# Value products per key block with 128 weight columns, and normalisation shared with the scalar engine, in the attention of a two-block layer

## The chip, the cores and the metric

One Trainium2 chip, one core of it. The metric is the time of one execution in device microseconds (us), the median of several runs. TensorE (PE) does the products, VectorE (DVE), the scalar engine (ACT) and GpSimd (POOL) the elementwise work, SyncE (SP) issues the DMAs. Reads of weights into TensorE are shown as PEld.

## The reference, cut to what matters

The input x has 512 rows (positions) and 1024 columns, all in float32. A first block (retention and differential attention) is followed by a second one, in which the change lies. The second block has eight heads "a" of dilated window attention and eight heads "b" of latent attention, each with values of 64 columns. Both come down to the same thing: scores of 512 queries against the keys up to their own position, a table of biases or of the causal mask added, softmax over the keys, and the product of the probabilities with the values.

```python
s = scores + table                       # (heads, 512, 512), causal
p = softmax(s, axis=-1)
o = einsum('hqk,khd->qhd', p, v)         # d = 64
mixed = concat([o_a * silu(z_a), o_b * silu(z_b)])
out = x + mixed @ w_out                  # 1024 x 1024
```

The softmax in the kernel subtracts the row's largest score, takes the exponential, sums it, and multiplies with the reciprocal of the sum. silu(z) is computed as 0.5 z (1 + tanh(z/2)); the kernel carries the 0.5 elsewhere.

## The kernel before, in words

**Numbers in two parts.** TensorE reads float32 operands here as a rounded format (fp32r). To keep float32 accuracy each operand is split into a high part (a rounded copy, made by the scalar engine) and a low part (what is left, made by VectorE by a subtraction): `split`, L266 to L268. A product of two such operands takes three matmuls, high x high, high x low and low x high: `mm3`, L304 to L307. Weights come by DMA as raw tiles and are split by the `Streamer` (L107 to L154): ACT makes the high part (L135), VectorE or GpSimd the low part (L137). GpSimd does it for the keys in `POOL_LO` (L51).

**The loop over steps.** In the second block a step is one tile of 128 queries (t = 0 to 3) of one head; the 16 heads come in the order of `SEQ` (L45): four "a", eight "b", four "a". In step s the loop (L1356 to L1366) issues

- `probs` (L1208): the scores of step s (t+1 blocks of 128 keys: width n of 128, 256, 384 or 512), their addition to the table with the row's extremum on VectorE (L1219), the exponential with its sum on ACT (L1222), the reciprocal (L1224) and the normalisation with a factor 0.5 on VectorE (L1225);
- at t = 1 and t = 2 the query and key stacks of the head after this one (`ready_q`, `ready_k`): transposes of normalised projections and their split into tiles of a ring with the tag "qk", 12 tiles long. A pair of "a" heads takes 2 + 4 tiles, a "b" head 4;
- `fill` up to half a step's share: pieces of dense work (projections, gates, the output projection) from a list, by a planned cost in columns against a due amount;
- `probs_T` (L1228) of step s-2: transposes of the normalised probabilities on TensorE (t+1 blocks), and their split into a high and a low tile per step;
- `fill` up to the full share;
- `weigh` (L1239) of step s-3: the value products. For each of the t+1 key blocks three matmuls with the values as weights (64 columns) and 128 columns of transposed probabilities, summed in a PSUM tile of 64 x 512 for the head. At t = 3 ACT copies that tile into one half of a 128 x 512 tile; after two heads `mix_in` (L1255) multiplies it with the gate and splits it for the output projection `project` (L1278).

TensorE's order in this loop is the order in which the program issues (`manual_schedule`, L891); the order on the other engines is laid by a planner at build time, which knows the dependencies but not the measured durations. Each engine works its queue in order. PSUM has three tiles for dense work (`ps_d`), two for transposes (`ps_t`), two for scores (`ps_s`) and one for value products (`ps_o`). One tile with the tag "th" is shared by the gates' tanh (L361) and the mix.

`mla_q` (L1070) makes the queries of the latent heads with a root mean square over 64 and over 32 columns per head; `mla_kv` (L1094) and `dil_v` (L1158) make the value tiles, a high and a low one each.

## Time and profile before

| | |
|---|---|
| time, median of 3 runs | 939.8 us (937.45 to 940.37) |
| the profiled execution, its own time | 939.06 us |
| its span in the trace | 936.7 us, 13702 instructions |
| TensorE (matmul) busy | 916.1 us, 98% of the span |
| weight loads (PEld) busy | 777.0 us, 83% |
| VectorE busy | 555.9 us, 59% |
| ACT busy | 452.7 us, 48% |
| GpSimd busy | 209.0 us, 22% |
| mean granted clock of TensorE | 0.996 of full speed |

The profile is of one execution. A row of the trace names the line of the kernel, the engine, the operation and the tiles written and read (out<-in). Matmuls are pipelined: the shown duration of one (0.22 us for 128 columns) is longer than the distance between the starts of two that follow each other, and the distance is what a product costs. The loop over steps fills the trace from about 705 us to 920 us; `project(2)` follows.

### The profile page before, as it was taken

Reading aid. Unit: us, or ns where it says so; the run is one execution under the profiler, and the core shown is the slowest. Engines: PE = TensorE matmul, PEld = TensorE weight load, DVE = VectorE, ACT = ScalarE, POOL = GpSimd, SP = SyncE. Lnnn points to the kernel's source line nnn. Section 1 sums busy time; section 2 is a strip of 40 time slices with the busy share of each in tenths; the row PEclk is TensorE's granted clock in tenths of the full one; section 3 lists DMA queues with packets and bytes.
Section 4 is the critical chain, followed back from the end, with each engine's and each line's share of the span. In section 5 each row is a group of like instructions: output and inputs, shape, how many; then the busy total and the mean of one; then the engine's idle time right before and its main releaser. Section 6 shows DMA issues by size and latency. Waiting matters only on the chain.

```text
span 936.7 us, 13702 instructions
## 1 busy us (share of the span) xinstructions
PE 916.1 (98%) x5113; PEld 777.0 (83%) x5113; DVE 555.9 (59%) x1223; ACT 452.7 (48%) x923; POOL 209.0 (22%) x236
## 2 busy tenths in 40 slices
PE   9999999999999999999999999999997999999998
PEld 6788887777888888888888888888996788999886
DVE  5443342347764555668665345344649897778884
ACT  5311331345555544666565433233545667666650
POOL 3001100116111133411310000132347453341100
PEclk9999999999999999999999999999999899999999
DMA  7474230322433423222332234633423121211412
GB/s 247 124 221 141 66 89 27 91 71 64 136 113 113 157 91 91 91 91 91 124 113 68 70 110 135 203 127 127 141 63 97 39 80 46 68 47 47 158 45 90
DMA packets 70099, 96.20 MB, mean 103 GB/s; under 512 B 5336, under 2 KB 46184, under 8 KB 70034
## 3 DMA queue, kind: packets, MB, share of 16 engines
q1 hardware_dynamic: 70034, 95.34, 32.5%
q8 instruction: 40, 0.66, 0.3%
q14 instruction: 25, 0.20, 0.1%
HBM read 86.91 MB, written 11.03 MB: 105 GB/s over the span
## 4 chain that ended last, share of the span: by engine, by line
PE 88%; DVE 6%; DMA 2%; ACT 2%; POOL 1%; issue 1%; SPq 0%; ACTq 0%; DVEq 0%
PE dps L305 9%; PE dps L307 9%; PE dps L306 9%; PE tps L305 7%; PE tps L307 7%; PE tps L306 7%; PE aps L305 2%; PE aps L306 2%; PE aps L307 2%; PE dop L823 2%; PE ppt L1231 2%; PE ops L305 2%; PE yps L307 2%; PE yps L305 2%; PE yps L306 2%; PE ops L306 2%
## 5 line engine op out<-in xcount | busy, mean ns | idle before, releaser
L137 DVE TENSOR_TENSOR wl<-wr,wh 128x1024 fp32r<-128x1024 f32 (+2 forms) x113 | 139.6, 1236 | 121.4 <-ACT wh L135 117.4
L135 ACT ACTIVATE wh<-wr 128x1024 fp32r<-128x1024 f32 (+1 forms) x132 | 137.7, 1043 | 147.4 <-DMA wr<-in_w_in_dram 46.9
L305 PE MATMUL dps<-h1h,wh 128*128 128x512 f32 x320 | 128.3, 401 | 0.0
L307 PE MATMUL dps<-h1h,wl 128*128 128x512 f32 x320 | 125.3, 392 | 0.0
L306 PE MATMUL dps<-h1l,wh 128*128 128x512 f32 x320 | 125.1, 391 | 0.0
L305 PE MATMUL tps<-wh,h1h 128*128 128x512 f32 x256 | 103.3, 404 | 3.0 <-ACT dqn L366 2.4
L307 PE MATMUL tps<-wh,h1l 128*128 128x512 f32 x256 | 101.3, 396 | 0.0
L306 PE MATMUL tps<-wl,h1h 128*128 128x512 f32 x256 | 100.2, 392 | 0.3 <-DVE wl L137 0.3
L307 PEld LDWEIGHTS dps<-h1h,wl 128*128 128x128 f32 x320 | 60.1, 188 | 13.0
L306 PEld LDWEIGHTS dps<-h1l,wh 128*128 128x128 f32 x320 | 60.2, 188 | 12.0 <-issue 0.5
L305 PEld LDWEIGHTS dps<-h1h,wh 128*128 128x128 f32 x320 | 60.2, 188 | 11.8
L305 PEld LDWEIGHTS tps<-wh,h1h 128*128 128x128 f32 x256 | 48.2, 188 | 14.7 <-ACT dqn L366 4.1
L307 PEld LDWEIGHTS tps<-wh,h1l 128*128 128x128 f32 x256 | 48.1, 188 | 11.0 <-DVE h1l L452 0.6
L305 PE MATMUL aps<-wh,h2h 128*128 128x256 f32 x192 | 56.9, 296 | 0.0
L306 PEld LDWEIGHTS tps<-wl,h1h 128*128 128x128 f32 x256 | 48.3, 189 | 9.9 <-DVE wl L137 0.7
L306 PE MATMUL aps<-wl,h2h 128*128 128x256 f32 x192 | 54.2, 282 | 0.0
L307 PE MATMUL aps<-wh,h2l 128*128 128x256 f32 x192 | 54.2, 282 | 0.0
L137 POOL TENSOR_TENSOR wl<-wr,wh 128x1024 fp32r<-128x1024 f32 (+2 forms) x19 | 42.9, 2261 | 40.3 <-ACT wh L135 32.7
L1222 ACT ACTIVATE p<-p,nm 128x128 f32<-128x128 f32 (+1 forms) x64 | 35.7, 557 | 22.6 <-DVE nm L1219 22.5
L794 DVE CUSTOM_DVE_ANT_0 p<-sp,tb 128x128 f32<-128x128 f32 (+3 forms) x64 | 29.0, 488 | 29.1 <-PE sp L302 28.9
L797 ACT ACTIVATE p<-p,nm 128x128 f32<-128x128 f32 (+3 forms) x64 | 35.5, 555 | 15.6 <-DVE nm L794 15.3
L251 POOL TENSOR_TENSOR gnrs<-gnrs,mhalf 128x8 f32<-128x8 f32 x24 | 41.8, 1747 | 1.7
(293 smaller groups left out, 2204.4 us busy)
## 6 DMA issues: line engine op xcount, KB each, us to landing
wr<-in_w_in_dram SPq DMA_DIRECT2D x92, 512.0 KB
wr<-in_w_out_dram SPq DMA_DIRECT2D x16, 512.0 KB
wr<-in_ret_w_o_dram SPq DMA_DIRECT2D x8, 512.0 KB
wr<-in_diff_w_o_dram SPq DMA_DIRECT2D x8, 512.0 KB
rep_dram<-rev_dram SPq DMA_DIRECT2D x8, 320.0 KB
y_dram<-my SPq DMA_DIRECT2D x8, 256.0 KB
my<-y_dram SPq DMA_DIRECT2D x8, 256.0 KB
m_dram<-mth SPq DMA_DIRECT2D x8, 256.0 KB
```

Source lines behind the costliest of these rows:

```text
L135: nc.scalar.activation(hi, raw, AF.Copy)
L137: eng.tensor_tensor(lo, raw, hi.bitcast(F32), op=ALU.subtract)
L251: nc.gpsimd.tensor_tensor(dst, dst, mhalf[:, :n], op=ALU.pow)
L305: nc.tensor.matmul(ps, lh, rh, start=start, stop=False)
L306: nc.tensor.matmul(ps, lh, rl, start=False, stop=False)
L307: nc.tensor.matmul(ps, ll, rh, start=False, stop=stop)
L794: nc.vector.tensor_tensor_reduce(p[:, :n], sp[:, :n], tables[head][:, S - n : S], scale=-1.0, scalar=3.0e38, op0=ALU.add, op1=ALU.min, acc ...
L797: nc.scalar.activation(p[:, :n], p[:, :n], AF.Exp, scale=-1.0, bias=nm, accum_out=den)
L823: nc.tensor.matmul(o_ps[:, t, :], aT[:, kt, :], vd[head // 4][:, kt, hc], start=kt == 0, stop=kt == t)
L1222: nc.scalar.activation(p[:, :n], p[:, :n], AF.Exp, scale=-1.0, bias=nm, accum_out=den)
L1231: nc.tensor.transpose(pt[:, kt, :], p[:, kt * P : (kt + 1) * P], ident)
```

## The change

- `weigh` works once per head instead of once per step. The value tile holds the high part in columns 0 to 63 and the low part in columns 64 to 127 of one weight block. For each of the four key blocks there are two matmuls, one with the high and one with the low probabilities, over all queries from that block on (512, 384, 256 and 128 columns). The PSUM tile has 128 rows; its two halves are added (ACT copies the one, VectorE adds the other).
- The transposed probabilities of a head go into one high and one low tile with 13 blocks, ordered so that the queries of one key block lie side by side. The pool has two such tiles.
- `weigh` stands ahead of `probs_T` in the step instead of at its end.
- The normalisation is done by ACT at even t and by VectorE at odd t; the factor 0.5 moves to `mix_in`.
- The ring "qk" of the second block has 9 tiles instead of 12.
- The low parts of the output weights wo2_00, wo2_01, wo2_10 and wo2_11 (six parts) go to GpSimd.
- `mla_q` scales the sums over 64 and 32 columns in two GpSimd operations instead of one on VectorE and one on GpSimd.

```diff
-POOL_LO = frozenset(FILL)
+POOL_LO = frozenset(FILL + ("wo2_00", "wo2_01", "wo2_10", "wo2_11"))
 QK_BUFS = 12
+QK_BUFS2 = 9
...
-                nc.vector.tensor_scalar(ss[:, 4:8], ss[:, 4:8], 2.0, None, op0=ALU.mult)
                 rs = stat.tile([P, 8], F32, name="urs", tag="urs")
-                rstd(rs, ss, 8, 1.0 / 64)
+                for c4, w in ((slice(0, 4), 64), (slice(4, 8), 32)):
+                    nc.gpsimd.tensor_scalar(rs[:, c4], ss[:, c4], 1.0 / w, EPS, op0=ALU.mult, op1=ALU.add)
+                nc.gpsimd.tensor_tensor(rs, rs, mhalf[:, :8], op=ALU.pow)
...
-            vh = wp.tile([P, NT, 4, 64], F32R, name="mvh", tag="vh")
-            vl = wp.tile([P, NT, 4, 64], F32R, name="mvl", tag="vl")
+            v = wp.tile([P, NT, 4, P], F32R, name="mv", tag="v")
...
-                split(vh[:, tt], vl[:, tt], ps[:, :, 64:128])
+                split(v[:, tt, :, 0:64], v[:, tt, :, 64:128], ps[:, :, 64:128])
...
-            vh = wp.tile([P, NT, 256], F32R, name="avh", tag="vh")
-            vl = wp.tile([P, NT, 256], F32R, name="avl", tag="vl")
+            v = wp.tile([P, NT, 4, P], F32R, name="av", tag="v")
             def done(tp, ps):
-                split(vh[:, 2 * tp : 2 * tp + 2, :], vl[:, 2 * tp : 2 * tp + 2, :], ps)
+                for i in range(2):
+                    split(v[:, 2 * tp + i, :, 0:64], v[:, 2 * tp + i, :, 64:128],
+                          ps[:, i].rearrange("p (h w) -> p h w", w=64))
...
-            nc.vector.tensor_scalar(p[:, :n], p[:, :n], rd, 0.5, op0=ALU.mult, op1=ALU.mult)
+            if t % 2:
+                nc.vector.tensor_scalar(p[:, :n], p[:, :n], rd, None, op0=ALU.mult)
+            else:
+                nc.scalar.activation(p[:, :n], p[:, :n], AF.Copy, scale=rd)
             return p
 
+        pT_now = []
         def probs_T(p, t):
+            if t == 0:
+                pT_now[:] = [wp.tile([P, 13, P], F32R, name=f"pT{a}", tag="pT") for a in "hl"]
             pt = ps_t.tile([P, NT, P], F32, name="ppt", tag="t")
             for kt in range(t + 1):
                 nc.tensor.transpose(pt[:, kt, :], p[:, kt * P : (kt + 1) * P], ident)
-            ph = wp.tile([P, NT, P], F32R, name="pTh", tag="pTh")
-            pl = wp.tile([P, NT, P], F32R, name="pTl", tag="pTl")
-            split(ph[:, : t + 1, :], pl[:, : t + 1, :], pt[:, : t + 1, :])
-            return ph, pl
+            to = slice(t, 4 * t + 1, 3)
+            split(pT_now[0][:, to, :], pT_now[1][:, to, :], pt[:, : t + 1, :])
+            return list(pT_now)
...
-        def weigh(kind, h, t, pT):
+        def weigh(kind, h, pT):
             kt = h // 2 + (4 if kind == "b" else 0)
-            if t == 0:
-                o_ps[0] = ps_o.tile([64, S], F32, name="oTp", tag="o")
-                if h % 2 == 0:
-                    o_sb[kt] = oT_pool.tile([P, S], F32, name="osb", tag="o")
-            vh, vl = values_of(kind, h)
-            cq = slice(t * P, (t + 1) * P)
-            for i in range(t + 1):
-                mm3(o_ps[0][:, cq], vh[:, i, :], vl[:, i, :], pT[0][:, i, :], pT[1][:, i, :], i == 0, i == t)
-            if t == NT - 1:
-                j = h % 2
-                nc.scalar.activation(o_sb[kt][64 * j : 64 * j + 64, :], o_ps[0], AF.Copy)
-                if j == 1:
-                    mix_in(kt)
+            if h % 2 == 0:
+                o_sb[kt] = oT_pool.tile([P, S], F32, name="osb", tag="o")
+            v = values_of(kind, h)
+            o_ps = ps_o.tile([P, S], F32, name="oTp", tag="o")
+            for i in range(NT):
+                for a in range(2):
+                    nc.tensor.matmul(o_ps[:, i * P :], v[:, i, :], flat(pT[a][:, 4 * i : 3 * i + 4, :]),
+                                     start=i == 0 and a == 0, stop=i == NT - 1 and a == 1)
+            j = h % 2
+            half = wp.tile([64, S], F32, name="ohalf", tag="th", bufs=1)
+            nc.scalar.activation(half, o_ps[64:128], AF.Copy)
+            nc.vector.tensor_tensor(o_sb[kt][64 * j : 64 * j + 64, :], o_ps[0:64], half, op=ALU.add)
+            if j == 1:
+                mix_in(kt)
...
-            nc.vector.tensor_tensor(tmp, zws[kt], o_sb[kt], op=ALU.mult)
+            nc.vector.scalar_tensor_tensor(tmp, zws[kt], 0.5, o_sb[kt], op0=ALU.mult, op1=ALU.mult)
...
             fill(s, 0.5)
+            if s > LAG:
+                pT = pT_of.pop(s - LAG - 1)
+                if steps[s - LAG - 1][2] == NT - 1:
+                    weigh(*steps[s - LAG - 1][:2], pT)
             if 0 <= s - LAG < n_steps:
                 pT_of[s - LAG] = probs_T(p_of.pop(s - LAG), steps[s - LAG][2])
             fill(s, 1.0)
-            if s > LAG:
-                weigh(*steps[s - LAG - 1], pT_of.pop(s - LAG - 1))
```

## Rows read from the trace of the kernel before

**Rows 1.** The page's chain that ended last, shares of the span by engine.

```profile
PE 88%; DVE 6%; DMA 2%; ACT 2%; POOL 1%; issue 1%; SPq 0%; ACTq 0%; DVEq 0%
```

**Rows 2.** Stages: length, busy us per engine, granted clock, DMA share, GB/s.

```profile
700.00:780.00 80.00, 71.91 (x461) 60.48 (x460) 71.15 (x212) 50.35 (x120) 45.56 (x49) 0.96 0.24 68
780.00:920.00 140.00, 139.85 (x1110) 126.49 (x1109) 110.41 (x289) 87.35 (x202) 32.07 (x30) 1.00 0.22 69
```

**Rows 3.** Waits of TensorE, 700 to 780 us: total us, times, longest.

```profile
PE ppt L1231 <- DVE pTl L268: 2.8, 2, 1.7
PE ppt L1231 <- DVE qst L283: 2.2, 1, 2.2
PE apt L1171 <- DVE pTl L268: 2.1, 1, 2.1
```

**Rows 4.** Stages of 5 us, columns as in rows 2.

```profile
720.00:725.00 5.00, 1.36 (x7) 0.88 (x7) 4.90 (x9) 2.25 (x5) 3.81 (x3) 0.95 0.44 124
725.00:730.00 5.00, 4.73 (x21) 3.95 (x22) 3.83 (x12) 2.15 (x5) 1.88 (x3) 0.50 0.26 89
730.00:735.00 5.00, 5.00 (x26) 4.06 (x25) 3.28 (x12) 3.41 (x10) 1.18 (x3) 0.87 0.21 52
```

**Rows 5.** Timeline of TensorE: start us, duration us, line, operation, count.

```profile
804.31 0.39 PE L307 MATMUL zps<-h2h,wl 128*128 128x512 f32 x1
804.53 0.22 PE L305 MATMUL oTp<-pTh,mvh 128*64 128x128 f32 x1
...
805.07 0.39 PE L305 MATMUL sp<-kh,qh 96*128 96x384 f32 x1
805.29 0.34 PE L306 MATMUL sp<-kl,qh 96*128 96x384 f32 x1
...
809.42 0.28 PE L305 MATMUL aps<-wh,h2h 128*128 128x256 f32 x1
809.54 0.28 PE L306 MATMUL aps<-wl,h2h 128*128 128x256 f32 x1
...
811.59 0.27 PE L305 MATMUL sp<-kh,qh 96*128 96x128 f32 x1
811.70 0.28 PE L306 MATMUL sp<-kl,qh 96*128 96x128 f32 x1
```

**Rows 6.** Groups by line and shape, 560 to 937 us: busy us, mean ns.

```profile
L137 DVE TENSOR_TENSOR wl<-wr,wh 128x1024 fp32r<-128x1024 f32 x25 | 31.4, 1258 | 14.2 <-ACT wh L135 14.1
L1222 ACT ACTIVATE p<-p,nm 128x384 f32<-128x384 f32 x16 | 9.8, 610 | 4.9 <-DVE nm L1219 4.8
L1225 DVE TENSOR_SCALAR p<-p,rd 128x128 f32<-128x128 f32 x16 | 8.8, 548 | 0.4
L267 ACT ACTIVATE pTh<-ppt 128x384 fp32r<-128x384 f32 x16 | 7.8, 486 | 7.9 <-PE ppt L1231 7.8
L1225 DVE TENSOR_SCALAR p<-p,rd 128x384 f32<-128x384 f32 x16 | 6.7, 420 | 0.3
L1222 ACT ACTIVATE p<-p,nm 128x128 f32<-128x128 f32 x16 | 6.3, 396 | 3.7 <-DVE nm L1219 3.7
L295 DVE TENSOR_TENSOR ksl<-apt,ksh 64x512 fp32r<-64x512 f32 x8 | 5.5, 688 | 0.5 <-ACT ksh L293 0.3
L267 ACT ACTIVATE pTh<-ppt 128x128 fp32r<-128x128 f32 x16 | 4.3, 269 | 4.5 <-PE ppt L1231 4.5
```

**Rows 7.** The same view of VectorE from 697 to 780 us.

```profile
L1225 DVE TENSOR_SCALAR p<-p,rd 128x128 f32<-128x128 f32 x6 | 4.3, 713 | 0.1
L1085 DVE TENSOR_SCALAR uss<-uss 128x4 f32<-128x4 f32 x8 | 1.7, 212 | 0.1
```

**Rows 8.** Timeline of all engines; in brackets the idle time before, and its releaser.

```profile
747.24 2.37 POOL L137 TENSOR_TENSOR wl<-wr,wh 128x1024 fp32r<-128x1024 f32 x1 [2.74 <-ACT wh L135]
...
747.78 1.91 DVE L1225 TENSOR_SCALAR p<-p,rd 128x128 f32<-128x128 f32 x1
...
750.21 0.66 PE L1231 MATMUL ppt<-ident,p 128*128 128x128 f32 x4 [1.66 <-DVE pTl L268]
```

More of the change, by code (lines that the diff above doesn't have):

```diff
@@ L286, in stack_q, with stack_k @@
         return out
-    def stack_k(pool, src):
+    def stack_k(pool, src, bufs=QK_BUFS):
         out = []
         for own, other in halves:
-            hi = pool.tile([P, S], F32R, name="ksh", tag="qk", bufs=QK_BUFS)
-            lo = pool.tile([P, S], F32R, name="ksl", tag="qk", bufs=QK_BUFS)
+            hi = pool.tile([P, S], F32R, name="ksh", tag="qk", bufs=bufs)
+            lo = pool.tile([P, S], F32R, name="ksl", tag="qk", bufs=bufs)
             nc.scalar.activation(hi[own], src[own], AF.Copy)
@@ L1114, in mla_kv @@
                 yield 3 * S
-            out.append((k, vh, vl))
+            out.append((k, v))
         def mla_prep(nm, src, h):
@@ L1120, in mla_prep @@
                 nc.tensor.transpose(pt[:96, tt, :], src[:, tt, h, :], ident)
-            hi = wp.tile([P, S], F32R, name=nm + "h", tag="qk", bufs=QK_BUFS)
-            lo = wp.tile([P, S], F32R, name=nm + "l", tag="qk", bufs=QK_BUFS)
+            hi = wp.tile([P, S], F32R, name=nm + "h", tag="qk", bufs=QK_BUFS2)
+            lo = wp.tile([P, S], F32R, name=nm + "l", tag="qk", bufs=QK_BUFS2)
             s96 = flat(pt[:96])
@@ new lines, in probs_T @@
+            split(pT_now[0][:, to, :], pT_now[1][:, to, :], pt[:, : t + 1, :])
+            return list(pT_now)
+        mix, zws, o_sb = {}, {}, {}
+        def weigh(kind, h, pT):
+            kt = h // 2 + (4 if kind == "b" else 0)
+            if h % 2 == 0:
[12 more added lines that the diff above has]
+                mix_in(kt)
```

18 lines of the change are left out of this document (7 added, 11 removed).

## The prediction

> **What bounds the kernel now.** I read the chain that ended last first: TensorE is 88% of it and VectorE 6% [rows 1]. So a TensorE time that goes is mostly a time that goes, and VectorE is the next to look at. The second block does not look the same throughout, which the table of stages shows [rows 2]. From 780 to 920 us TensorE is busy 139.85 of 140 us: it is the bound there, with VectorE at 110.4 and the scalar engine at 87.4. From 700 to 780 us it is busy only 71.9 of 80 us, and VectorE at 71.2 is as full. In that stretch TensorE stands mostly behind VectorE: 2.8 us for low parts of transposed probabilities, 2.2 us for a query stack, 2.1 us for a low part again [rows 3]. The worst place is 720 to 725 us, where TensorE is busy 1.36 of 5 us; behind it the granted clock is 0.50 for 5 us and 0.87 for the next 5 [rows 4], that is 1.2 GHz for part of the time. At reduced clock 5 x (0.05 + 0.50 + 0.13) = 3.4 us of work are lost.
>
> **The value products.** Before, a head has 10 blocks of keys and queries with 3 products each, all 128 columns wide with 64 weight columns. They start 0.06 us apart: nine of them lie between 804.53 and 805.07 [rows 5]. 480 of them make 28.8 us. After, a head has 8 products with 128 weight columns, 512, 384, 256 and 128 columns wide, each width twice. Wide products start 0.22 us apart at 512 columns (804.31 to 804.53) and 0.12 at 256 (809.42 to 809.54); 0.17 for 384 lies halfway between. For 128 columns with 128 weight columns I take the score products at 811.59 and 811.70, 0.11 apart: there the weights are wider, and the product is not shorter than at 256 columns [rows 5]. That is 2 x (0.22 + 0.17 + 0.12 + 0.11) = 1.24 us a head and 19.8 us for 16 heads. The saving is 9.0 us.
>
> A hand-over goes as well. The first score product behind a value product takes 0.22 us at 384 columns (805.07 to 805.29) where 0.17 is due, so 0.05 more [rows 5]; at 128 columns there is nothing to see. This holds in three of four steps, 48 times, 2.4 us. After, score products follow wide dense products. The transposes behind the last, narrow value product of a head may get such a loss instead: 16 times 0 to 0.1 us. I count 2 us net. **TensorE loses 11 us of work** (9.4 to 11.4 by these bounds).
>
> **What VectorE loses and gets.** The normalisation of the 128- and 384-wide steps goes to the scalar engine: 8.8 + 6.7 = 15.5 us [rows 6]. Six low parts of the output weights go to GpSimd, 6 x 1.26 = 7.6 us [rows 6]. New is one add of two halves per head; the nearest row is the subtraction of 64x512 with one input in PSUM, 0.69 us, so 16 x 0.69 = 11 us. The net is 12 us less. In 700 to 780 alone six 128-wide normalisations take 4.3 us [rows 7], some five 384-wide ones 2.1, the eight small scalings of the query sums 1.7 [rows 7]; against this stand four to five adds, 3.1 us. VectorE gets about 5 us shorter there. TensorE's saving in that stretch is about 80/220 of 11, that is 4 us, and since VectorE gets shorter by at least as much, I count it in full.
>
> **One stall should go.** At 747.24 GpSimd starts a weight subtraction of 2.37 us; the 128-wide normalisation on VectorE starts at 747.78, takes 1.91 us and ends with it, and the transposes behind it wait 1.66 us [rows 8]. The Trainium skill, "SBUF — State Buffer", section "SBUF: two separate sides", says that VectorE and GpSimd share one pair of ports under an exclusive lock held for a whole instruction, and that a VectorE operation in a two-port mode or with two SBUF inputs blocks against it. By that rule six more GpSimd subtractions speak against the change; this trace agrees with the lock. From the rows alone: six times up to 2.37 us is 14 us of possible VectorE waiting, against 7.6 us taken off; in 780 to 920 VectorE has 29.6 us idle [rows 2], so I take 0 on the path. The stalled operation of [rows 8] is one of those that move to the scalar engine. Late next is VectorE's low part, which it delayed. I count 1.5 us.
>
> **What is added elsewhere.** The scalar engine gets 32 normalisations. The transposed copy of the same shape bounds them below (0.27 and 0.49), the exponential above (0.40 and 0.61) [rows 6], so 12 to 16 us; I take 16, as the exponential reads the same tile with a per-partition operand. It has 52.6 us idle in 780 to 920 and 29.6 in 700 to 780 [rows 2], so nothing on the path. Such a normalisation waits for VectorE's reciprocal, and the next exponential and high parts queue behind it (the rival below). The scalar copy of half the products takes the place of the old copy of them; it shares a single buffer with the gates and the mix, and the next head's products need the bank only four steps later, a step being 3.3 us (two steps from 805.07 to 811.59) [rows 5]: nothing. The head's products now come half a step sooner behind the last transposes, with about 1.6 us less for the copies between: 0 to 1.6 us per head; I take 0.5 us in all, since in 780 to 920 TensorE waits only 0.15 us. The first value tile is split in four pieces instead of two ahead of the first step: two more fixed shares of 0.16 us (0.27 at 128 columns less the slope of 0.11 per 128 columns) [rows 6], 0.3 us. The ring of nine instead of twelve tiles fits the six new tiles of a pair beside three live ones; only at the step from latent heads to the last pair is it one short, and a tile waits for one step's scores: 0 to 2 us, I take 0.3, since only the second head of the pair needs it. No DMA is moved, but raw weights of the six parts come free 1.1 us later on GpSimd, and SP's later loads and tables with them; a table is asked for two steps, 6.6 us, ahead: nothing. The extra GpSimd scalings of the query sums replace a VectorE operation: nothing. The factor 0.5 rides on a multiplication that was there: nothing.
>
> **Sum:** 939.06 (the profiled execution, 936.7 of span and 2.4 around it) - 11 - 1.5 + 0.5 + 0.3 + 0.3 = 927.7; I say **927.5**. The profiled execution lies 0.7 us below the median of 939.8.
>
> **The rivals.**
> - The stall at 720 us goes too. For it: VectorE is shorter there. Against it: what delays VectorE at 720 stays on VectorE. It is worth 3.64 + 0.27 us of idle time up to 730 us [rows 4] and the 3.4 us of reduced clock: 7.3, so 920.
> - A new stall of that kind. VectorE's and GpSimd's orders are laid anew, and one collision as in [rows 8] at a tight place costs 2 us idle, or with the clock 7.3: 935. Any operation left on VectorE that collides can be the place.
> - VectorE still sets the pace in 700 to 780, and the 4 us of TensorE's saving and the 1.5 us there are lost: 933.
> - Slower: the scalar engine's queue. At each even step it stands at the normalisation until the reciprocal is there, and the next exponential and high part come late. If TensorE loses 0.36 us per even step (11.6/32), the gain is gone; with 0.6 us, 32 x 0.6 = 19, it is 947. For it: in-order queue, and a VectorE that at times is 1.9 us late [rows 8]. Against: a third of the scalar engine's time is idle, and two steps, 6.6 us, lie between scores and transposes.
>
> **How the numbers follow.** Chances: the forecast 0.43, the stall at 720 gone 0.20, a new stall 0.17, no gain in 700 to 780 0.08, the scalar queue 0.08, and 0.04 that two of the small losses join and end near 939. A measurement of this kernel tells about 0.3%, 2.8 us, from no change. All but the last two and a part of the new stalls (0.03) are faster: 0.85; same 0.07; slower 0.08. The range from 918 to 936.5 takes in the first four cases with the bounds of their costs and leaves out some 0.15.
>
> **What would show it.** Right: value products of 128 records, 512 wide ones 0.22 us apart, some 20 us in all; TensorE busy nearly all of 780 to the end; no wait of 1.7 us near 747; normalisations of 128 columns on the scalar engine at about 0.40 us. Wrong: TensorE waiting at many even steps for high or low parts with the scalar engine near 90% (the slower rival); a second stretch with the clock at 0.5; or value products of 512 columns farther apart than 0.23 us, which would take the first term away.

## The result, and the profile after

The changed kernel takes 934.2 us (median of 4 runs, 932.72 to 936.12), the kernel before in the same comparison 940.09 us (937.45 to 942.29). The ratio is 0.994, with a 95% interval from 0.9926 to 0.9954: 5.9 us faster, a little less than half of the 12.6 us by which the forecast lay below the same 940.09. The time lies inside the range that was given, and on the side that was given 0.85.

The profiled execution after is the slowest of its four, 936.12 us with a span of 934.2. Busy time by engine and the chain that ended last, of the page of the changed kernel (the chain answers to [rows 1]):

```profile
PE 908.6 (97%) x4761; PEld 768.3 (82%) x4761; DVE 548.0 (59%) x1197; ACT 466.5 (50%) x959; POOL 227.2 (24%) x250
PE 85%; DVE 7%; ACT 2%; DMA 2%; POOL 1%; issue 1%; SPq 0%; ACTq 0%; DVEq 0%; POOLq 0%
```

TensorE's part of the chain fell, VectorE's rose. The two stages of [rows 2] after the change, with the same columns:

```profile
700.00:780.00 80.00, 71.56 (x389) 60.96 (x389) 69.42 (x200) 58.55 (x138) 51.05 (x58) 0.98 0.24 68
780.00:920.00 140.00, 134.96 (x869) 120.35 (x867) 107.62 (x278) 96.81 (x227) 46.26 (x36) 1.00 0.22 68
```

From 780 to 920 us TensorE was idle for 0.15 us before; now it is idle for 5.04 us. So in the stage where TensorE was the only bound it is no longer quite that.

The two traces must not be compared from their starts. The first block is the same in both, and yet the first score product of the second block starts at 702.98 us before and at 706.12 after (more on this at the end). So I take each span from that product on. The second block as one stretch, in the view by windows, first before:

```profile
702.98:936.70 233.72, 222.15 (x1608) 194.80 (x1608) 185.97 (x504) 136.85 (x320) 74.72 (x73) 0.98 0.23 71
```

and after:

```profile
706.12:934.20 228.08, 210.66 (x1257) 183.01 (x1256) 179.64 (x479) 150.36 (x354) 92.70 (x90) 0.99 0.24 74
```

The stretch is 5.6 us shorter, which agrees with the medians. In it TensorE's busy time fell by 11.5 us (222.15 to 210.66), and its idle time rose by 5.9 us (233.72 - 222.15 = 11.6 to 228.08 - 210.66 = 17.4). This has one flaw: the first product itself waited in the kernel before, and that wait lies ahead of the stretch. The first two score products, before:

```profile
702.98 0.33 PE L301 MATMUL sp<-ksh,qst 128*128 128x128 f32 x1 [0.68 <-POOL ksh L294]
703.54 0.33 PE L302 MATMUL sp<-ksl,qst 128*128 128x128 f32 x1 [0.23 <-POOL ksl L296]
```

and after:

```profile
706.12 0.26 PE L302 MATMUL sp<-ksh,qst 128*128 128x128 f32 x1
707.61 0.33 PE L303 MATMUL sp<-ksl,qst 128*128 128x128 f32 x1 [1.23 <-POOL ksl L297]
```

With these 0.7 us counted the idle time rose by 5.2 us. This is the whole result: **the work went as forecast, and about half of it came back as waiting.** The waits of TensorE from 690 us to the end, after the change (total us, times, longest; [rows 3] is the same view of the first of the two stages before):

```profile
PE oTp L1254 <- DVE pTl L269: 3.7, 2, 2.1
PE ppt L1238 <- DVE pTl L269: 3.3, 4, 2.6
PE ppt L1238 <- DVE rd L1223: 2.7, 1, 2.7
PE apt L1173 <- DVE pTl L269: 1.4, 3, 0.7
PE sp L303 <- POOL ksl L297: 1.2, 1, 1.2
PE mpt L1121 <- DVE ql L273: 0.9, 1, 0.9
PE ops L306 <- DVE part L1303: 0.3, 1, 0.3
PE oTp L1254 <- ACT pTh L268: 0.3, 1, 0.3
```

The first line is new in kind: the value products (oTp) wait for the low parts of the transposed probabilities (pTl), twice, 3.7 us in all; with the last line the value products wait 4.0 us. Before, value products waited 0.2 us in the whole block.

The value products of one head in TensorE's timeline, to be read against [rows 5]:

```profile
804.66 0.40 PE L1254 MATMUL oTp<-pTh,mv 128*128 128x512 f32 x1
804.90 0.39 PE L1254 MATMUL oTp<-pTl,mv 128*128 128x512 f32 x1
805.13 0.34 PE L1254 MATMUL oTp<-pTh,mv 128*128 128x384 f32 x1
805.30 0.34 PE L1254 MATMUL oTp<-pTl,mv 128*128 128x384 f32 x1
805.48 0.28 PE L1254 MATMUL oTp<-pTh,mv 128*128 128x256 f32 x1
805.60 0.28 PE L1254 MATMUL oTp<-pTl,mv 128*128 128x256 f32 x1
805.71 0.22 PE L1254 MATMUL oTp<-pTh,mv 128*128 128x128 f32 x1
805.77 0.28 PE L1254 MATMUL oTp<-pTl,mv 128*128 128x128 f32 x1
805.88 0.29 PE L1238 MATMUL ppt<-ident,p 128*128 128x128 f32 x1
```

From 804.66 to 805.88 they take 1.22 us; the prediction had 1.24.

Where the waits come from is seen at four places. Each fence is the timeline of all engines, start and duration first. The stall of [rows 8] did not go; it moved to a 512-wide normalisation, one of those left on VectorE:

```profile
745.86 2.36 POOL L138 TENSOR_TENSOR wl<-wr,wh 128x1024 fp32r<-128x1024 f32 x1 [1.11 <-ACT wh L136]
745.91 2.60 DVE L1225 TENSOR_SCALAR p<-p,rd 128x512 f32<-128x512 f32 x1
...
749.63 0.91 PE L1238 MATMUL ppt<-ident,p 128*128 128x128 f32 x4 [2.58 <-DVE pTl L269]
```

GpSimd starts 0.05 us ahead, and the normalisation, 0.49 us when nothing is in its way, takes 2.60. Behind it a low part is late and the transposes wait 2.58 us. The longest wait, at 723 us, stands behind an instruction held in the same way, a query operation that takes 0.41 us alone and 2.60 here:

```profile
719.24 2.64 POOL L138 TENSOR_TENSOR wl<-wr,wh 128x1024 fp32r<-128x1024 f32 x1
719.56 2.60 DVE L1090 TENSOR_TENSOR mq<-mq,urs 128x256 f32<-128x256 f32 x1
...
723.72 0.63 PE L1238 MATMUL ppt<-ident,p 128*128 128x128 f32 x4 [2.72 <-DVE rd L1223]
```

At 868 us two of the low parts that the change moved to GpSimd do the same in front of value products:

```profile
862.74 4.77 POOL L138 TENSOR_TENSOR wl<-wr,wh 128x1024 fp32r<-128x1024 f32 x2 [3.16 <-PE ppt L1238]
...
865.96 1.70 DVE L1225 TENSOR_SCALAR p<-p,rd 128x256 f32<-128x256 f32 x1
...
867.91 0.68 DVE L269 TENSOR_TENSOR pTl<-ppt,pTh 128x512 fp32r<-128x512 f32 x1
...
868.64 0.50 PE L1254 MATMUL oTp<-pTl,mv 128*128 128x512 f32 x1 [1.58 <-DVE pTl L269]
```

And at 905 us nothing is held, but the low part stands in VectorE's queue behind a weight low part and an addition of the output projection:

```profile
901.83 0.57 ACT L268 ACTIVATE pTh<-ppt 128x512 fp32r<-128x512 f32 x1
...
902.55 1.22 DVE L138 TENSOR_TENSOR wl<-wr,wh 128x1024 fp32r<-128x1024 f32 x1
...
903.69 0.68 DVE L1303 TENSOR_TENSOR part<-part,ops 128x512 f32<-128x512 f32 x1
904.28 0.69 DVE L269 TENSOR_TENSOR pTl<-ppt,pTh 128x512 fp32r<-128x512 f32 x1
...
905.02 0.50 PE L1254 MATMUL oTp<-pTl,av 128*128 128x512 f32 x1 [2.07 <-DVE pTl L269]
```

The high part is there at 902.40, the low part at 904.97. Before, TensorE waited only 0.15 us from 780 to 920 us; the value products stood half a step later and needed the low parts only then.

### The profile page after: what moved, and what is told of

Same layout as the page of the kernel before. It is cut to its first block, busy times and chain, and to the rows that moved or that the text cites. A ratio compares the mean times of both kernels' runs of the same rounds, so it can differ in the third digit from the quotient of the medians.

```text
span 934.2 us, 13019 instructions
## 1 busy us (share of the span) xinstructions
PE 908.6 (97%) x4761; PEld 768.3 (82%) x4761; DVE 548.0 (59%) x1197; ACT 466.5 (50%) x959; POOL 227.2 (24%) x250
## 4 chain that ended last, share of the span: by engine, by line
PE 85%; DVE 7%; ACT 2%; DMA 2%; POOL 1%; issue 1%; SPq 0%; ACTq 0%; DVEq 0%; POOLq 0%
PE dps L306 9%; PE dps L308 9%; PE dps L307 9%; PE tps L306 7%; PE tps L308 7%; PE tps L307 7%; PE aps L306 2%; PE aps L308 2%; PE aps L307 2%; PE dop L824 2%; PE oTp L1254 2%; PE yps L308 2%; PE yps L307 2%; PE yps L306 2%; PE ops L306 2%; PE ops L307 1%
## 5 line engine op out<-in xcount | busy, mean ns | idle before, releaser
L138 DVE TENSOR_TENSOR wl<-wr,wh 128x1024 fp32r<-128x1024 f32 (+2 forms) x107 | 131.4, 1229 | 121.1 <-ACT wh L136 117.4
L306 PEld LDWEIGHTS dps<-h1h,wh 128*128 128x128 f32 x320 | 60.1, 188 | 11.9
L138 POOL TENSOR_TENSOR wl<-wr,wh 128x1024 fp32r<-128x1024 f32 (+2 forms) x25 | 57.6, 2308 | 47.0 <-ACT wh L136 42.5
L307 PEld LDWEIGHTS tps<-wl,h1h 128*128 128x128 f32 x256 | 48.6, 190 | 10.2 <-DVE wl L138 0.8
L1221 ACT ACTIVATE p<-p,nm 128x128 f32<-128x128 f32 (+1 forms) x64 | 35.6, 557 | 17.2 <-DVE nm L1218 17.1
L798 ACT ACTIVATE p<-p,nm 128x128 f32<-128x128 f32 (+3 forms) x64 | 35.5, 556 | 15.6 <-DVE nm L795 15.2
```

The lines of the kernel that those rows point to most:

```text
L138: eng.tensor_tensor(lo, raw, hi.bitcast(F32), op=ALU.subtract)
L306: nc.tensor.matmul(ps, lh, rh, start=start, stop=False)
L307: nc.tensor.matmul(ps, lh, rl, start=False, stop=False)
L798: nc.scalar.activation(p[:, :n], p[:, :n], AF.Exp, scale=-1.0, bias=nm, accum_out=den)
L1221: nc.scalar.activation(p[:, :n], p[:, :n], AF.Exp, scale=-1.0, bias=nm, accum_out=den)
```

## The experiments

Three theories were put to the test. **A**: the new place of the value products, directly behind the last low parts, is what costs. **V**: VectorE has too much work, and TensorE waits for it one way or another. **L**: GpSimd's long low parts hold VectorE instructions, and this makes the large waits. Theories B, C, O, S, I, P and Q in single runs are rivals or variants, explained where they stand.

All runs in one table. Ratios are to the kernel before on the same chip, with the 95% interval. The other columns are of the profiled execution, from the first score product of the second block to the end: length, TensorE's idle time in it, waits of the value products, and "held". Held is worked out from VectorE's timeline from 690 us on: for each form of instruction, what its instances take beyond the quickest quarter, where that is over 0.12 us, summed. What TensorE waits ahead of the first score product is in neither length nor idle time: nothing in the changed kernel and in e1 to e8, 0.7 us in the kernel before, e9 and e12 to e16, 1.4 in e11 and 1.7 in e17.

| kernel | time us | ratio | stretch | idle | oTp waits | held |
|---|---|---|---|---|---|---|
| before | 940.1 | 1 | 233.7 | 11.6 | 0.2 | 12.3 |
| changed | 934.2 | 0.994 (0.9926, 0.9954) | 228.1 | 17.4 | 4.0 | 13.1 |
| e1 products later | 939.48 | 0.9994 (0.9977, 1.0011) | 234.8 | 20.4 | 2.2 | 18.9 |
| e2 normalisation all on VectorE | 946.78 | 1.007 (1.0056, 1.0083) | 240.3 | 25.1 | 5.9 | 23.6 |
| e3 wo2 low parts on VectorE | 936.36 | 0.9955 (0.9941, 0.9968) | 227.7 | 17.5 | 2.3 | 9.9 |
| e4 all but the value products | 939.61 | 0.9985 (0.9975, 0.9996) | - | - | - | - |
| e5 high products first | 938.76 | 0.9963 (0.9951, 0.9976) | 231.1 | 19.4 | 3.3 | 14.1 |
| e7 normalisation all on ACT | 933.5 | 0.9914 (0.99, 0.9927) | 227.6 | 17.2 | 2.6 | 8.0 |
| e8 without the addition | 937.15 | 0.995 (0.9937, 0.9964) | 230.6 | 18.7 | 5.2 | 14.3 |
| e9 GpSimd in quarters | 930.48 | 0.9878 (0.9864, 0.9892) | 224.5 | 13.8 | 3.4 | 7.1 |
| e11 before, in quarters | 935.67 | 0.995 (0.9937, 0.9963) | 228.0 | 7.6 | 0.0 | 6.6 |
| e12 e9 and e7 | 933.05 | 0.9921 (0.9902, 0.994) | 225.8 | 13.0 | 2.6 | 5.2 |
| e13 e9 and e2 | 934.84 | 0.994 (0.9922, 0.9957) | 227.1 | 15.2 | 3.0 | 10.1 |
| e14 e9 and e1 | 929.72 | 0.9891 (0.9875, 0.9907) | 222.3 | 11.8 | 1.1 | 6.7 |
| e15 e9, all wo2 on GpSimd | 930.29 | 0.9891 (0.9877, 0.9904) | 222.6 | 11.9 | 2.0 | 7.0 |
| e16 e15 and e1 | 928.41 | 0.9877 (0.9863, 0.989) | 220.3 | 10.2 | 0.0 | 5.7 |
| e17 GpSimd in eighths | 933.53 | 0.9935 (0.9914, 0.9956) | 223.7 | 12.9 | 3.3 | 4.2 |

TensorE's busy time in the stretch (length less idle) is 210.1 to 215.2 us in every kernel with the new products and 220.4 and 222.2 in the two with the old ones. So everything that differs among the variants is waiting, and clock behind waiting.

**e1: the value products back at the end of the step**, behind the second half of the fill.

```diff
-            if s > LAG:
-                pT = pT_of.pop(s - LAG - 1)
-                if steps[s - LAG - 1][2] == NT - 1:
-                    weigh(*steps[s - LAG - 1][:2], pT)
+            pT = pT_of.pop(s - LAG - 1) if s > LAG else None
+            ends = s > LAG and steps[s - LAG - 1][2] == NT - 1
...
             fill(s, 1.0)
+            if ends:
+                weigh(*steps[s - LAG - 1][:2], pT)
+                if s - LAG < n_steps:
+                    pT_of[s - LAG] = parts_T(pt, steps[s - LAG][2])
```

> Edit: the value products of a head go back to the end of the step (half a step later), with everything else as in the changed kernel; the split of the next head's first tile follows them. Theory A (the products now come too soon behind the low parts of the head's last tile): the two waits of 1.6 and 2.1 us of value products for low parts shrink to under 0.7 us each, the time falls by 2 to 4 us against the changed kernel, to 930 to 932. Theory B (the scalar engine's normalisation makes the chain late) and theory C (the GpSimd low parts of the output weights hold VectorE up): the waits stay or move to transposes, and the time is within 1.5 us of the changed kernel's.

The waits of the value products fell to two of 1.0 and 1.1 us (A had under 0.7 each), but the time went up to that of the kernel before, which none of the three theories had. The order laid anew brought another collision, in e1's timeline:

```profile
761.08 2.35 POOL L138 TENSOR_TENSOR wl<-wr,wh 128x1024 fp32r<-128x1024 f32 x1
761.15 2.56 DVE L1090 TENSOR_TENSOR mq<-mq,urs 128x256 f32<-128x256 f32 x1 [1.26 <-POOL urs L1089]
...
765.39 0.63 PE L1236 MATMUL ppt<-ident,p 128*128 128x128 f32 x4 [3.67 <-DVE rd L1223]
```

An operation that takes 0.41 us alone takes 2.56, the transposes wait 3.67 us, and in the 5 us behind them the granted clock is 0.66. So A could not be judged by this run alone.

**e2: all normalisations on VectorE.**

```diff
-            if t % 2:
-                nc.vector.tensor_scalar(p[:, :n], p[:, :n], rd, None, op0=ALU.mult)
-            else:
-                nc.scalar.activation(p[:, :n], p[:, :n], AF.Copy, scale=rd)
+            nc.vector.tensor_scalar(p[:, :n], p[:, :n], rd, None, op0=ALU.mult)
```

> Edit: all normalisations on VectorE, the rest as in the changed kernel. Theory B: the scalar engine's part in the chain was what cost, and the time falls by 2 us or more. Theory A: nothing about the distance between low parts and products changes, VectorE gets 15 us more work; the time is equal or up to 4 us longer than the changed kernel's, with longer waits for low parts.

By the ratios 12 us slower than the changed kernel and 6.6 slower than before: B fails, and the loss is far larger than A had it. With long low parts on GpSimd the new value products do not pay without the shared normalisation. V and L both explain that, since VectorE has more to do and holds rise from 13.1 to 23.6 us. e13 was made to tell them apart.

**e3: the low parts of the output weights back on VectorE** (`POOL_LO = frozenset(FILL)`).

> Edit: the low parts of the six output weight parts back on VectorE, the rest as in the changed kernel. Theory C: the 1.6 us wait near 868 us, behind a VectorE normalisation of 1.7 us beside GpSimd subtractions, goes, and the time falls by 1.5 to 2 us. Theory A: VectorE gets 7.6 us more work in the stretch where it is late, and the waits of value products grow; equal or up to 3 us longer.

The wait at 868 us is gone, so it was these low parts on GpSimd. Others took its place (two waits for the reciprocal, 4.1 us in all, where the changed kernel has one of 2.7), and by the ratios the time rose by 1.4 us, within the intervals, where C had asked for a gain of 1.5 to 2 us; the waits of value products fell from 4.0 to 2.3 us, where A had them grow.

**e4: all of the change but the value products**: the old products with the shared normalisation, the low parts on GpSimd and the new scaling of the query sums.

> Edit: the kernel before with the other parts alone (normalisation shared, low parts on GpSimd, factor 0.5 moved, GpSimd scalings of the query sums), the value products as before. If the value products carry the gain, as forecast (11 of 11.6 us): within 2 us of the kernel before. If the relief of VectorE matters more than was counted: 3 us or more faster than the kernel before. If the scalar engine's queue costs (theory B): slower than the kernel before by 2 us or more.

The rest alone is worth 1.4 us, within the 2 us that were put for it if the value products carry the gain; B fails again. The traced execution took 2341.59 us; its trace is not used, and it is not in the median of the table. With e2: the products with the normalisation left on VectorE lose, the relief of VectorE without them gains a little, and only both together gain 6.

**e5: the four high products ahead of the four low ones.**

```diff
-            for i in range(NT):
-                for a in range(2):
+            for a in range(2):
+                for i in range(NT):
```

> The changed kernel with the eight value products of a head issued as four with the high parts and then four with the low parts, instead of high and low in turn. Nothing else is touched. In the changed kernel two heads have a wait of the second value product for the low parts of the last step (1.58 us at 868.6 and 2.07 us at 905.0). Theory A (the value products stand directly behind VectorE's last low part, and that is what was mis-sized): the four high products take 1.23 / 2 = 0.62 us and now run inside these waits, so each falls by 0.62 us, and the heads that wait for a few tenths lose that too: 1.2 to 2 us faster than the changed kernel, ratio to the kernel before 0.992 to 0.993. Theory V (VectorE is late as a whole, and what TensorE does not wait for here it waits for at the next turn): the two waits fall by 0.62 us each, others grow by as much, and the time stays within 0.5 us of the changed kernel (ratio 0.994).

The two waits became 1.24 and 1.71 us, 0.35 shorter each instead of 0.62, and the kernel as a whole 2 us slower: a collision that cost at most 0.9 us in the changed kernel (a query operation at 763.7) now had transposes behind it that waited 3.33 us. Neither theory foresaw that. Nothing but the order of eight products per head was changed; that tenths of a microsecond then decide which instructions meet is the likely reason, not a tested one.

**e7: all normalisations on ACT**, those of odd t too.

> The changed kernel with all normalisations of the second block on the scalar engine, those of the odd steps too: 16 of 0.73 us and 16 of 0.49 us leave VectorE (19.5 us), and as many of about 0.7 and 0.5 us come to the scalar engine (its busy time in 780 to 920 goes from 97 to about 109 us of 140, in 700 to 780 from 59 to about 66 of 80). Theory V (TensorE waits for VectorE as a whole; putting 13 us back on it cost 11.6 us): the waits of the stretch, 13.5 us in all, shrink by half or more, 5 to 9 us faster than the changed kernel, ratio to the kernel before 0.985 to 0.989. Theory L (only the normalisations that GpSimd holds up matter): the 2.58 us wait at 749.6 and the 1.58 us wait at 868.6 go, the rest stays: 3 to 4 us faster, ratio 0.990 to 0.991. Theory S (the scalar engine's queue is the next bound, because the exponentials and the high parts stand behind the new work): no gain or a loss of up to 5 us, ratio 0.994 to 1.000, with waits of TensorE named ACT.

Against the changed kernel the ratio fell from 0.994 to 0.9914, while the stretch stayed within 0.5 us (227.6 to 228.1). Normalisations of 19.5 us left VectorE (its busy time in the stretch fell from 179.6 to 167.8 us, the held time by 5 us), and TensorE's idle time changed by 0.2 us. V asked for 5 to 9 us; it fails here. The ratio is near what L asked for, but not in the way that it was put: the waits of 2.58 and 1.58 us went, and others came (2.28 us at 721, 1.44 at 764). No wait above 0.5 us names ACT, so S fails as well.

**e8: without the addition of the halves**; ACT copies rows 0 to 63, the products of the values' high parts. The contribution of the low parts of the values is left out of the computation.

```diff
-            half = wp.tile([64, S], F32, name="ohalf", tag="th", bufs=1)
-            nc.scalar.activation(half, o_ps[64:128], AF.Copy)
-            nc.vector.tensor_tensor(o_sb[kt][64 * j : 64 * j + 64, :], o_ps[0:64], half, op=ALU.add)
+            nc.scalar.activation(o_sb[kt][64 * j : 64 * j + 64, :], o_ps[0:64], AF.Copy)
```

> The changed kernel without the addition of the two halves of a head's output on VectorE: the scalar engine copies the upper 64 rows straight to the output tile. Left out of the computation is the contribution of the low parts of the values. It takes 16 additions of 0.68 us (10.9 us) off VectorE, each right behind a copy for which VectorE waited 10.5 us in all. Theory V (VectorE's work as a whole is what TensorE waits for): 4 to 8 us faster than the changed kernel, ratio to the kernel before 0.986 to 0.990. Theory O (what counts is what stands directly ahead of a low part at the few places where VectorE is late; the addition is mostly beside other work): within 1.5 us of the changed kernel, ratio 0.9925 to 0.9955.

Additions of 10.9 us left VectorE, and there is no gain; the ratio is within O's band. V fails a second time: the amount of VectorE's work is not what TensorE waits for.

**e9: each low part on GpSimd in four instructions** over a quarter of the columns.

```diff
-        eng.tensor_tensor(lo, raw, hi.bitcast(F32), op=ALU.subtract)
+        w = n // 4 if eng is nc.gpsimd else n
+        for c in range(0, n, w):
+            eng.tensor_tensor(lo[:, :, c : c + w], raw[:, :, c : c + w],
+                              hi[:, :, c : c + w].bitcast(F32), op=ALU.subtract)
```

> The changed kernel with each low part that GpSimd makes of a weight tile issued as four instructions over a quarter of the columns instead of one of 2.4 us. Same work, so VectorE has the same instructions. Theory L (a running GpSimd low part holds a VectorE normalisation that meets it until GpSimd's instruction ends, and this makes the largest waits left): a hold ends within 0.6 us instead of up to 2.4 us, the normalisations at 746 and 865 take 0.7 to 1.2 us instead of 2.60 and 1.70 us, and the waits of 2.58 and 1.58 us lose 1 to 1.5 us each: 2 to 3 us faster than the changed kernel, ratio to the kernel before 0.991 to 0.992. Theory V (the amount of VectorE's work and its order): no change beyond 0.5 us, ratio 0.994. A loss of 1 to 2 us would say that the fixed part of a GpSimd instruction, or more holds of a shorter kind, cost more than the long ones.

The largest gain of a single edit: 0.9878, 5.8 us below the changed kernel by the ratios. L asked for 2 to 3, and the trace shows no more than that: the stretch is 3.6 us shorter, 2.9 with the wait ahead of the stretch. The same place as at 868 us above, in e9's timeline:

```profile
856.14 5.67 POOL L140 TENSOR_TENSOR wl<-wr,wh 128x256 fp32r<-128x256 f32 x8 [3.16 <-issue]
...
859.37 0.47 DVE L1228 TENSOR_SCALAR p<-p,rd 128x256 f32<-128x256 f32 x1
...
860.82 0.50 PE L1257 MATMUL oTp<-pTl,mv 128*128 128x512 f32 x1 [0.36 <-DVE pTl L272]
```

GpSimd is busy longer (5.67 us where it was 4.77), but the normalisation takes 0.47 us instead of 1.70, and the wait is 0.36 instead of 1.58. The wait at 749 is gone (one of 1.48 us stands later, at 758). The one at 905 is not: 2.06 us. Nor is the one at 723: 2.59 us.

**e11: the kernel before in quarters**, the same edit.

> The kernel before, with GpSimd's low parts of the weights as four instructions over a quarter of the columns. Theory L (the half of the forecast that did not come went into VectorE instructions that GpSimd's long low parts hold, in places where only the changed kernel waits for them): in the kernel before, TensorE's waits in 700 to 780 that stand behind a held VectorE instruction are those of 1.66 and, in part, 2.15 and 1.19 us, so it gains 2 to 4 us (ratio 0.996 to 0.998), and the change on top of short holds is worth 8 to 9 us. Theory I (short holds are an improvement by themselves that has nothing to do with the change): it gains as much as the changed kernel did, 5 to 6 us (ratio 0.994), and the change on top of short holds is worth the same 6 us as without.

L, as put for this run, is not borne out: the kernel before gains 4.7 us, nearer to what I asks for. In its trace the gain lies in the first five heads (70.0 to 64.3 us from the first score product of the first head to that of the sixth). So holds cost both kernels about the same, and shortening them is an improvement by itself. It does not explain why the change gave half: with short holds in both, the change is worth 0.9878/0.995 = 0.993, 6.8 us, and TensorE idles 13.8 us with it and 7.6 without (14.5 and 9.0 with the waits ahead of the stretch).

**e12: e9 and e7 together.**

> The changed kernel with the low parts in quarters and with all normalisations of the second block on the scalar engine. Theory L (holds are the price, and moving the odd normalisations away helped by 2.5 us because five of them were held, 6.0 us in all): with short holds the move has little left to win, within 1.5 us of the quarters alone, ratio to the kernel before 0.986 to 0.989. Theory V (the amount of work on VectorE): 19.5 us less work gives 3 to 6 us more than the quarters alone, ratio 0.981 to 0.985.

The stretch is 225.8 us where e9 has 224.5, the idle time 13.0 where e9 has 13.8; by the ratio it is slower than both theories had it. 19.5 us off VectorE again give nothing.

**e13: e9 and e2 together.**

> The changed kernel with all normalisations on VectorE (which alone was 11.6 us slower than the changed kernel, with 23.6 us of holds against 13.1) and the low parts in quarters. Theory L (that loss was holds): most of it goes, 1 to 4 us slower than the quarters alone, ratio to the kernel before 0.989 to 0.992. Theory V (that loss was VectorE's amount of work, 13 us more of it): it stays, 8 to 12 us slower than the quarters alone, ratio 0.996 to 1.001.

By the ratios all normalisations on VectorE now cost 5.8 us where they cost 12 with long holds; in the stretch 2.6 us where they cost 12.2. The ratio lies between the two bands, so by time the run decides for neither; in the stretch most of e2's loss was holds.

**e14: e9 and e1 together.**

> The changed kernel with the value products back at the end of the step (which alone was 4 to 5 us slower than the changed kernel, though the waits of the value products themselves became shorter) and the low parts in quarters. Theory L (that loss was a held VectorE instruction at 761 and the wait of 3.7 us behind it): the loss goes, within 1.5 us of the quarters alone or faster, since the value products wait less: ratio to the kernel before 0.985 to 0.989. Theory P (the place by itself costs: the transposes that now stand ahead of the value products wait for the probabilities): 3 to 5 us slower than the quarters alone, ratio 0.991 to 0.993.

With the long holds out of the way, later value products are no loss any more: the ratio equals that of e9 within the intervals, and the stretch is 2.2 us shorter, with 1.1 us of waits of the value products instead of 3.4. The loss of e1 was its collision, not the place; P fails.

**e15: e9, with the last two output weight tiles' low parts on GpSimd too** (`"wo2_20", "wo2_21"` added to `POOL_LO`). This takes the 1.22 us instructions away from ahead of the low part at 905 us.

> The changed kernel with low parts in quarters, and with the low parts of the last two output weight tiles, which VectorE makes (1.22 us each, four of them, two at 900.6 and 902.6 us of the changed kernel), moved to GpSimd as well. Theory Q (the wait of the value products for the low parts at 905, 2.07 us in the changed kernel and 2.06 us with quarters alone, is VectorE's queue: one 1.22 us weight low part and one 0.68 us addition stand ahead of the probabilities' low part): the wait falls to 0.8 us or less and the time by 1.2 to 1.5 us against quarters alone, ratio to the kernel before 0.986 to 0.987. Rival (the probabilities come late to that place anyway, because the scalar engine's two copies of these weights stand ahead of the high parts): the wait stays above 1.5 us and the time within 0.5 us, ratio 0.988.

TensorE's timeline at the place that was 905 us:

```profile
900.31 0.50 PE L1257 MATMUL oTp<-pTl,av 128*128 128x512 f32 x1 [0.64 <-DVE pTl L272]
```

2.06 us became 0.64: Q was right on the wait, which was VectorE's queue. The stretch fell by 1.9 us; the ratio, 0.9891 against 0.9878, did not fall and meets neither band, within the intervals of both runs.

**e16: e15 with the value products later.**

> The same two edits with the value products back at the end of the step. Theory Q: the last wait of the value products there, 1.14 us, falls to a few tenths, about 1 us faster than later products with quarters (ratio to the kernel before 0.989), so 0.987 to 0.988; TensorE waits in the second block for no more than 7 us in all. Rival: no change, 0.989.

No wait of a value product is left; the ratio is within Q's band, and the waits that the view lists come to 7.2 us, where Q had no more than 7. TensorE's idle time is 10.2 us and less than in the kernel before, and the stretch is the shortest of all, 220.3 us: 13.4 less than before. The time is 928.41 us, ratio 0.9877. Against e9 it cannot be told apart by time; both beat the changed kernel, whose interval theirs do not touch.

**e17: eighths instead of quarters.**

> The changed kernel with GpSimd's low parts of the weights as eight instructions over an eighth of the columns (1024 columns: 128 in each). Theory L (what a hold costs goes with how long one GpSimd instruction runs; quarters took the holds of VectorE from 13.1 to 7.1 us): holds fall further to about 4 us, the time by up to 1 us against quarters (ratio to the kernel before 0.987 to 0.988). If the number of holds grows as they become shorter, or GpSimd's fixed cost of an instruction makes the low parts late (its busy time grew from 48 to 57 us by quartering), the time is 1 to 3 us longer than with quarters, 0.989 to 0.991.

Holds fell to 4.2 us, as L had it, and the stretch by 0.8 us, but that is only because 1.7 us of waiting lie ahead of the stretch instead of 0.7: with them it is 225.4 us, and 225.1 in e9. By the ratios the kernel is 5.4 us slower than e9, with intervals that do not touch; both bands are missed. Its six executions fall in two groups: three of 929.8 to 931.9 us, as long as those of e9, with a mean granted clock of 0.996 to 0.998, and three of 935.2 to 936.4 us with 0.991 to 0.993. So the loss goes with the clock; why it falls more often here, or whether that is chance, is open.

## Why the prediction was right or wrong

**The work of TensorE: right.** Forecast was a loss of 11 us (9.0 of products, 2 of hand-overs). Measured are 11.5 us of busy time. Head against head, where the clock is full in both, it is 0.68 us a head: from the sixth head's first score product to the sixteenth's it took 127.5 us before and 123.2 after, with 2.5 us of new waits in it, so (127.5 - 123.2 + 2.5) / 10. Times 16 this is 10.9 us; the rest of the 11.5 is less time at reduced clock. The spacings, 1.22 us a head, were as put. One bound was added up wrong: 9.0 + 2.4 - 1.6 is 9.8, not 9.4; nothing hangs on it.

**The step that failed is the waits.** In the sum they came to -0.4 us (1.5 gained at one stall; 0.5, 0.3 and 0.3 lost). Measured are +5.2 us of idle time: 3.8 at value products, 0.0 from 720 to 770 us, 1.1 at other transposes from 780 us on, 0.3 at the start of the block. Term by term:

- "The head's products now come half a step sooner behind the last transposes ... I take 0.5 us in all." This is the largest miss: 4.0 us (3.7 for low parts, 0.3 for high parts) where it was 0.2, nearly all in two heads of sixteen. My reason was that TensorE waited only 0.15 us from 780 to 920 before. But that was a number of the old order, in which a value product had a half step of slack; the edit took just that slack away. The bound that I had worked out myself, 0 to 1.6 us a head, would have allowed it. e14 and e16 confirm the place in the traces: with the products back at the end and short holds the waits of value products are 1.1 and 0.0 us, and the stretch is 2.2 and 2.3 us shorter than in e9 and e15. By the ratios neither difference is clear of the noise.
- "One stall should go ... I count 1.5 us." The stall of [rows 8] left the 128-wide normalisation and came back at a 512-wide one, as 2.58 us. All waits between 720 and 770 us together were 7.2 us before (2.15, 2.19, 1.66, 1.19) and are 7.2 after (2.72, 0.53, 0.26, 2.58, 0.22, 0.91): nothing was gained. Held time stayed as a whole, 12.3 and 13.1 us; it is not a property of the instruction that was hit, but of how long GpSimd's instructions are. e9 shows the price: the same kernel with short ones idles 3.6 us less (3.0 with the wait ahead of the stretch).
- GpSimd's six new low parts, "0 on the path": one of the two waits of the value products, 1.58 us, was theirs (gone in e3, 0.36 in e9). The rule of the Trainium skill that the prediction weighed ("SBUF — State Buffer", section "SBUF: two separate sides": an exclusive lock for a whole instruction) agrees with all of these rows; here it did cost, and e9 and e11 show that the length of one instruction counts.
- "The first value tile is split in four pieces ... 0.3 us": the first two score products of the block wait 1.23 us together where they waited 0.91. That is the 0.3, but for the parts of a key stack that GpSimd writes; no row shows that the value tile is the reason, so the agreement may be luck.
- The 1.1 us at transposes from 780 us on (0.20, 0.20 and 0.70 us) were in no term. They too wait for low parts.

**VectorE: half right.** It was to get 12 us shorter; from 560 us to the end it got 8.0 us shorter (260.15 to 252.13). The groups of the changed kernel by shape, from 690 us on:

```profile
L1225 DVE TENSOR_SCALAR p<-p,rd 128x512 f32<-128x512 f32 x16 | 11.7, 730 | 0.4
L1259 DVE TENSOR_TENSOR osb<-oTp,ohalf 64x512 f32<-64x512 f32 x16 | 10.9, 683 | 10.6 <-ACT ohalf L1258 10.5
L1225 DVE TENSOR_SCALAR p<-p,rd 128x256 f32<-128x256 f32 x16 | 7.8, 487 | 0.3
L1090 DVE TENSOR_TENSOR mq<-mq,urs 128x256 f32<-128x256 f32 x8 | 7.3, 919 | 1.0 <-POOL urs L1089 1.0
```

The addition takes 683 ns, as taken from [rows 6]. But the 512-wide normalisations, 484 ns on average before, now take 730, and the query operation 919 instead of 641: the holds that left with the moved instructions landed on those that stayed (mean times; held time as a whole was 12.3 and is 13.1 us). Taking more off VectorE gave nothing in any case (e7, e8 and e12); putting all normalisations back cost 2.6 us in the stretch even with short holds (e13).

**The rivals.** The second one is what came nearest: "A new stall of that kind ... Any operation left on VectorE that collides can be the place", 935, chance 0.17. It named the mechanism at 749 and, with the low part as the thing that is late, at 868. That its 935 lies next to 934.2 is luck: it was one collision at 7.3 us, and what came is several waits of 0.3 to 2.7 us, one of them (905) behind no collision. The doubt that stood against the first rival, that what delays VectorE at 720 stays on VectorE, was right: an operation of 0.21 us took 1.74 beside a GpSimd low part at 717.5 us before, the query operation 2.60 at 719.6 after. That VectorE sets the pace from 700 to 780 (933) is near in time, but by e7 and e8 not for its reason. The slower rival, ACT's queue, did not come: no wait of TensorE for ACT in the second block is above 0.3 us.

What stays open: e9's gain in time (5.8 us) is larger than in the stretch of its trace (2.9 to 3.6), and e12, e15 and e17 do not show in time what their stretches show. The granted clock differs from execution to execution by as much (below), and one trace per kernel does not settle it. With short holds in both kernels the waits that remain with the change are partly VectorE's queue (e15) and partly the place (e14, e16); what part each has by time is within the noise. Several edits move other instructions too (e5), so a single wait that comes or goes in one of these traces is weak evidence by itself.

## What to carry to other kernels

When an edit takes work off the bounding engine and moves an operation closer behind its inputs, price the slack that it gives up, from the timeline of the producers in each round of the loop; idle time measured in the old order says nothing on it. A stall by contention is not removed by moving the instruction that was hit; shorten the instruction that holds, or it hits the next one. Once the bound engine is relieved, part of the gain can come back as waiting (here about half); look for it in the rounds where rare work (weights, a projection) stands in the same queue.

## What the runs showed of the hardware that was not expected

**Shorter instructions on GpSimd paid although GpSimd was busy longer.** Quarters raised GpSimd's busy time in the stretch (92.70 to 102.14 us) and cut the held time of VectorE from 13.1 to 7.1 us. The edit alone took 4.7 us off the kernel before and 5.8 off the changed one. Eighths raised the busy time to 115.95 us and brought nothing more.

**The same wait costs the clock in one execution and not in another.** In the first block, which is the same program in both kernels, TensorE waits 1.93 us (before, to 175.63 us) and 1.74 us (after, to 176.07) for a normalised tile. Stages of 5 us, columns as in [rows 2]; before:

```profile
175.00:180.00 5.00, 4.37 (x19) 3.64 (x20) 2.65 (x5) 0.58 (x2) 1.20 (x2) 1.00 0.71 209
```

and after:

```profile
175.00:180.00 5.00, 3.93 (x10) 3.12 (x11) 3.26 (x6) 1.02 (x2) 1.20 (x2) 0.66 0.56 167
```

Before, the clock stays at 2.4 GHz; after, it is 1.2 GHz for part of the stage, and what follows is 1.5 us later. The same happens near 640 us (granted clock 0.91 and 0.75 after, 1.00 before), where waits of 1.9 and 0.5 us lie (1.7 and 0.5 before), and 1.8 us are lost. e9 and e14 came through both places almost without loss of time, e12 lost 1.6 and 1.8 us. This, and 0.6 us at the very start, is why the profiled execution after is 4.0 us late at 695 us and 3.1 us at 706. It may be a good part of the 3 to 5 us between runs of one kernel; in e17 the long executions are those with the lower mean clock, but no kernel was traced twice. It reaches into the stretch as well: behind the 2.07 us at 905 the changed kernel's clock stays at 1.00, behind the 2.06 us at 897 in e9 it is 0.83 from 895 to 905 us. So a stall of 2 us has a price of its own length and, in some executions, 1.5 to 1.8 us more.
